# Matmuls on 36, 48 or 64 rows of the array take all 128, over zeros, and a head pair's value products go together

## The chip, the cores and the metric

The kernel runs on one core of a Trainium2 chip. Its time is the device time of one execution in microseconds; the profile is one execution, recorded by the hardware profiler. TensorE (PE) multiplies, with its weight loads shown apart (PEld), VectorE (DVE), ScalarE (ACT) and GpSimd (POOL) do the rest, and SyncE (SP) issues the transfers. Each takes its own instructions in order.

## What is computed

A stack of three layers for 512 tokens of 1024 features in float32: two layers with dilated attention (8 heads of 64) beside an mLSTM (4 heads of 128), then one with a state-space scan (SSD, 16 heads of 64), an attention to the best 128 keys that an indexer (4 heads of 64) picks, and a pooling branch. All have a feed-forward part. Cut to what the change touches:

```
# first block, per head and pattern of dilation
s = einsum('bnqhd,bnkhd->bnhqk', qb, kb) * (Dh ** -0.5)       # scores, Dh = 64
p = exp(s - max(s)); l = sum(p)
o = einsum('bnhqk,bnkhd->bnqhd', p, vb) / l                   # value products
# mLSTM: gate pre-activations mi, mf (4 columns each) of z = h @ w_in + b_in, running maximum m_t
p = exp(dmat - m_t[..., None]) * einsum('bhcld,bhcsd->bhcls', q, k)
# second block
lmat = exp(where(causal, a_cs[l] - a_cs[s], -inf))            # SSD, per head
score = einsum('bqhs,bqh->bqs', relu(einsum('bqhd,bsd->bqhs', qi, ki)), wi * idx_scale)
logits = einsum('bqhgd,bqkhd->bqhgk', qb, ksel) * att_scale   # ksel: keys of the top 128 scores
```

## The kernel before

All products run on TensorE in the float32r format, with each operand split into a first part `h` and a rest `l`; a weight product is three matmuls (`wh` by `h`, `wh` by `l`, `wl` by `h`: lines 280 to 282, or 319 to 321 where the weights move). The backbone is a stream of weight chunks of 128x1024: a transfer (SP queue) into `wr`, the first part on ScalarE (line 250), the rest on VectorE (line 256) or for some on GpSimd (line 254), then 24 matmuls of 512 columns, then an evacuation of the PSUM tile `pb`.

Everything else runs beside that stream as generators: after each K tile of the stream `tick()` lets every generator go on by a fraction of a step (RATE, 0.437 steps a tick for the first attentions, 0.704 for the last), up to its next `yield`. This sets the order in which the program is traced; the tile layer's scheduler then sets the order on each engine. Nothing is reordered at run time.

The pieces that the change touches:

- *Scores.* A head has 64 dimensions. `stack_q` makes a tile A with the head's first part in 64 rows and its rest in the other 64; `stack_k` makes B with the keys' first part in both halves (ScalarE writes one half, line 426, GpSimd copies it to the other, line 427) and writes the keys' rest into the head's own 64 rows of C (line 428). Both heads of a pair share one C. `dots` (lines 434 and 435) is then A by B over 128 rows plus A by C over the head's 64 rows, into one PSUM tile S of n = 128, 256, 384 or 512 columns. Four pairs of heads, two heads each and four query blocks give 32 score pairs in each of the three attentions. The indexer calls `dots` for four heads and the query blocks 1 to 3.
- *After the scores.* VectorE reduces S (line 450), ScalarE takes exp (451), VectorE scales (452, 453), TensorE transposes (462, one 128x128 piece per key block) into PSUM, and VectorE or ScalarE copies to `pt` (470, 468). S, PT, and the other side tiles share two PSUM buffers.
- *Values.* Line 479, for each of four key blocks and both heads: 128 rows, 64 of the output's partitions per head, 512, 384, 256 or 128 columns, with a `yield` after each key block and one split at the end.
- *Broadcasts.* A row held in two float32r parts is spread over 128 partitions by a product with a selecting column (`selr`): `nM` and `fr` of the mLSTM on 36 rows (lines 949 and 1030, per head), `bs` of the SSD on 48 rows (line 1467 per head, 1479 per pair of heads).
- *Gates.* The chunk of the few gate columns carries both parts of the weights side by side; per K tile there is one product on all 128 outputs (line 720) and one on 64 of them (719, 722).

Of the kernel before, what the change touches and what calls it, by code (L numbers as in the profile page):

```python
# [10 lines left out]
F32 = mybir.dt.float32  # L11
F32R = mybir.dt.float32r
# [8 lines left out]
NB = 4  # L21
# [6 lines left out]
# columns between the key blocks of a head's transposed weights  # L28
PTS = 384

# columns of w_in, first block
AQ, AK, AV, MQ, MK, MV, MO, MI, MF, GA, GB = 0, 512, 1024, 1536, 2048, 2560, 3072, 3584, 3588, 3592, 4616
# columns of w_in, second block
# [12 lines left out]
# ---------------------------------------------------------------- constants that depend on shapes alone  # L46
# [31 lines left out]
# ---------------------------------------------------------------- parameters laid out by partition  # L78
# [51 lines left out]
# steps of the work beside the weights per step of the weight stream  # L130
RATE = {"att1": 0.437, "rec": 0.556, "ssd": 0.5, "idx": 0.45, "att2": 0.704, "pool": 0.219}
# gates of the attention's branch that go before its projection
AHEAD = 2
# steps between what one engine prepares and what another one does with it
PAUSE = {"cs": 2, "lf": 5, "cols": 2, "fr": 10, "sum": 1}
# tiles of features that go side by side at the start of a product
LEAD = {"conv": 0, "mo": 0, "ga": 0, "gb": 2, "pa": 2, "pb": 0, "z": 0, "qi": 2, "kv": 2, "q": 2, "br": 2, "up": 2, "u": 2}
# part of the weight chunks whose second part GpSimd works out
SHARE = {"none": 0, "qk": 0.0, "conv": 0.3, "gates": 0.1, "conv2": 0.4, "z": 0.0, "br": 0.2}
# parts in which the first chunks come, and the products before them  # L140
FIRST = [(0, 256), (256, 1024)]
WARM = 36
# the residual's tile before whose preparation the angles of the rotary embedding come
ROPE = 5
# the last product's tiles of features that go over all tokens at once
TAIL = 4
# how far the norms' chains go before what was traced ahead of them
# [3 lines left out]
class Build:  # L151
# [16 lines left out]
    # ---- tiles  # L168
# [26 lines left out]
    # ---- work beside the weight stream: generators that go on a little at each step of it  # L195
# [22 lines left out]
    # ---- a stream of weight chunks, in the order of their use, each split into two float32r parts  # L218
    def chunk(self, key, l, rows, cs, keep=False):
        """one chunk's parts by K tile; with keep, in tiles that last."""  # L220
# [39 lines left out]
    def split(self, src, w=None, n=T):  # L260
        """float32r parts of src (times a per-partition w)."""
        nc = self.nc
        h, lo = self.t("h", F32R), self.t("l", F32R)
        if w is None:
            nc.scalar.activation(h[:, :n], src, AF.Copy)  # L265
            nc.vector.tensor_tensor(lo[:, :n], src, h[:, :n].bitcast(F32), ALU.subtract)  # L266
        else:
            a = nc.scalar.activation(h[:, :n], src, AF.Copy, scale=w)
            b = nc.vector.scalar_tensor_tensor(lo[:, :n], src, w, h[:, :n].bitcast(F32), ALU.mult, ALU.subtract)
            self.last_split = (a, b)  # L270
        return h, lo

    # ---- out[features, tokens]: tiles = [(psum, (wh, wl), first column, columns)], over the K tiles of xs
# [12 lines left out]
    def lin_cols(self, key, l, tiles, xs, evac, lead=0, K0=0):  # L286
        """tiles: lists of up to 128 columns of the weight; evac(j, psum) takes each out. The first
        `lead` tiles go side by side over K, where the last of xs come late."""
# [19 lines left out]
    def lin_tok(self, key, l, cs, xs, evac):  # L308
        """out[tokens, 512 features] by token block."""
# [17 lines left out]
    # ---- a per-token column [128, NB] as rows over all partitions, in PSUM  # L327
# [14 lines left out]
    def colsum(self, tiles):  # L342
        """sums over the partitions (and tiles) by token, as a column [128, NB]."""
# [13 lines left out]
    def rsqrt(self, src, n, scale, tag):  # L357
        """1 / sqrt(src * scale + EPS), or 1 / sqrt(src), by Newton's iteration"""
# [30 lines left out]
    def log1pexp(self, src, dst, rows, n, tag):  # L389
        """dst = max(src, 0) + log1p(exp(-|src|))"""  # L390
# [21 lines left out]
    # ---- heads of 64: [h; l] of one operand against [h; h] of the other over 128 rows, and h against l  # L412
    def stack_q(self, a, x):
        """head x of a pair's tile: its float32r part in its own rows, the rest in the other half."""
# [7 lines left out]
    def stack_k(self, a, x, C):  # L422
        nc = self.nc
        r, o = slice(64 * x, 64 * x + 64), slice(64 - 64 * x, 128 - 64 * x)
        B = self.t("B", F32R)
        nc.scalar.activation(B[r], a[r], AF.Copy)
        nc.gpsimd.tensor_copy(B[o], B[r].bitcast(F32))
        nc.vector.tensor_tensor(C[r], a[r], B[r].bitcast(F32), ALU.subtract)
        return B

    def dots(self, ps, A, B, C, x, c0, n):
        """ps[128, n] = products of the head's columns c0 .. c0 + 128 of A with the first n of B"""
        r = slice(64 * x, 64 * x + 64)
        self.nc.tensor.matmul(ps[:, :n], A[:, c0 : c0 + P], B[:, :n], start=True, stop=False)  # L434
        self.nc.tensor.matmul(ps[:, :n], A[r, c0 : c0 + P], C[r, :n], start=False, stop=True)  # L435

    # ---- softmax attention over key blocks 0..I; heads in pairs that share an output tile
    def attention(self, pairs, prep, V, bias, out):
# [4 lines left out]
        def score(it, x):  # L443
# [3 lines left out]
            self.dots(sp, *qk[pair, x], x, I * P, n)  # L447
# [24 lines left out]
        def value(it):  # L472
            """both heads' products with the values, by key block for all the queries from it on"""
            pair = it[0]
            yp = self.pw.tile([P, T], F32, name=self.name("yp"), tag="yp", bufs=1)
            for J in range(NB):
# [3 lines left out]
                yield  # L480
            out.append(self.split(yp))

# [26 lines left out]
    def conv_silu(self, ps, rbc, nb, w, cb):  # L509
        """silu(causal conv over 4 tokens of ps * rbc, after tokens of the value nb; w [128, 4]).  # L510
        A bias b of the tokens comes as nb = -b, with b times the sum of w in cb."""
# [17 lines left out]
    def setup(self):  # L529
# [6 lines left out]
        # column 127 of ones: its slices are one-hot rows for sums over the partitions  # L536
# [3 lines left out]
        # the tensor engine's clock rises with use: products of zeros until the first operands are there  # L540
# [3 lines left out]
        # the first chunks come by parts: K tiles 0 and 1, then the rest  # L544
# [56 lines left out]
    def norm_in(self, w):  # L601
        """the residual's tiles times w, split, and the sums of their squares."""
# [12 lines left out]
    # ---------------------------------------------------------------- a layer of the first block  # L615
    def hybrid(self, l, xs, acc):
# [11 lines left out]
        # attention: queries and keys with rotary embedding, values by token  # L628
# [44 lines left out]
        C = [None] * 4  # L673

        def prep(i, x):
            if x == 0:
                C[i] = self.t("C", F32R)
            return self.stack_q(qk[i], x), self.stack_k(qk[4 + i], x, C[i]), C[i]
# [16 lines left out]
        # mLSTM: queries, keys, values, gates  # L695
# [13 lines left out]
        # input and forget gates: few columns, so both parts of the weights go as one stationary  # L709
# [7 lines left out]
        for k, (xh, xl) in enumerate(xs):  # L717
            if k > 0:
                nc.tensor.matmul(ps[0:64, :], wh[:, k, 0:64], xl, start=False, stop=False)
            nc.tensor.matmul(ps, wh[:, k, :], xh, start=k == 0, stop=k == 7)  # L720
            if k == 0:
                nc.tensor.matmul(ps[0:64, :], wh[:, k, 0:64], xl, start=False, stop=False)
# [24 lines left out]
        # gated projections of both branches  # L747
# [26 lines left out]
        # the mLSTM's heads, normalised and gated  # L774
# [27 lines left out]
        # feed-forward: relu(y R)^2 = R^2 relu(y)^2, and R^2 goes by token, so it comes in after the second product  # L802
# [33 lines left out]
    def residual(self, w, scale=None):  # L836
        """adds to the residual (times the row of a scale), and prepares its tiles for the next norm by w"""
# [24 lines left out]
    def mlstm(self, it, lf, mqk, mv, res):  # L862
# [3 lines left out]
        # log_sigmoid(f) = -softplus(-f), in columns by token  # L866
# [14 lines left out]
        # within blocks of 128 tokens: b = cumsum(lf); u = i - b; M = running max of u with the carry  # L881
# [15 lines left out]
        # rows of -M, split, for broadcasts  # L897
        yield
        nM = self.t("nM", F32R)[:36]
# [6 lines left out]
        # columns: m = b + M by token, and u with the block decays before query block I  # L906
# [34 lines left out]
        def rowsum(c, src, first, last):  # L941
            """adds the column sums of src to row c of dn"""
# [4 lines left out]
        for h in range(4):  # L947
            bc = self.ps("mbc")
            nc.tensor.matmul(bc, self.sel[0:36, h : h + 1].to_broadcast([36, P]), nM, start=True, stop=True)
# [45 lines left out]
        # rows of den and of num^2 as columns by token  # L995
# [11 lines left out]
        # r = 1 / max(|den|, exp(-m)); the head's norm: r / sqrt(r^2 mean(num^2) + eps)  # L1007
# [14 lines left out]
        fr = self.t("fr", F32R)[:36]  # L1022
# [5 lines left out]
        def out(h):  # L1028
            ps = self.ps("fb")
            nc.tensor.matmul(ps, self.sel[0:36, h : h + 1].to_broadcast([36, P]), fr, start=True, stop=True)  # L1030
# [4 lines left out]
    # ---------------------------------------------------------------- the second block  # L1035
    def second(self, xs, st):
# [4 lines left out]
        # norm of a norm: x' = x R fin with R = 1 / sqrt(a + eps), a the mean of x^2, and x' R' with  # L1041
        # R' = 1 / sqrt(R^2 b + eps), b the mean of (x fin)^2: R R' = 1 / sqrt(b + eps (a + eps))
# [40 lines left out]
        # SSD inputs  # L1083
# [10 lines left out]
        # the SSD branch beside its gate z and the projections of the attention  # L1094
# [39 lines left out]
        # merge of the gated branches  # L1134
# [36 lines left out]
        def pooled(j):  # L1171
            if j == 4:
# [9 lines left out]
        kC = self.t("C", F32R)  # L1182
        kB = [self.stack_k(kv[0], x, kC) for x in range(2)]
# [3 lines left out]
                lambda i, x: (self.stack_q(q[i], x), kB[x], kC),  # L1187
# [19 lines left out]
        # feed-forward, silu(a) * b  # L1207
# [23 lines left out]
        # the last tiles of the last part and the final norm go by halves of the tokens: the first half's norm  # L1231
        # beside the second's products
# [57 lines left out]
    # means over the last 2, 4, 8, 16 tokens, less the token itself, mixed by group  # L1290
    def pool(self, u, yp):
# [5 lines left out]
        # room in the tiles that the attention's transposed weights take later  # L1297
# [302 lines left out]
```

## Time and profile before

| | before |
|---|---|
| median of 3 runs | 2516.99 us (2515.29 to 2517.63) |
| span of the profiled execution | 2514.6 us |
| TensorE busy, share | 2487.1 us, 99% |
| weight loads busy, share | 1944.9 us, 77% |
| VectorE | 1458.1 us, 58% |
| ScalarE | 1006.3 us, 40% |
| GpSimd | 426.5 us, 17% |

The span runs from the first to the last instruction of the profiled execution; the timed runs hold a little more than it. Matmuls are pipelined: one starts before the one ahead of it has ended, so the sum of their durations is larger than the busy time, and what one costs is the step from its start to the next start. A weight load may start while the matmul ahead of it still runs.

### The profile page before, as it was taken

The page shows a single profiled execution, that of the slowest core. Times are in us where ns is not written, and L with a number is a line of the kernel's source. Part 1 is how long each engine was busy: PE and PEld are TensorE (multiplying, and loading weights), DVE is VectorE, ACT ScalarE, POOL GpSimd, SP SyncE. Part 2 cuts the span into 40 slices and gives each one's busy share as a digit, 9 for nine tenths or more (in the row PEclk, how much of TensorE's full clock was granted, in tenths as well). Part 3 has the DMA queues.
Part 4 walks back from the last instruction along what each step waited for, and adds up shares of the span by engine and source line. Part 5 has one row for each costly group of instructions (what it writes and reads, how often), then busy time and mean ns, then how long its engine had stood idle before and what let it go on. Part 6 is the DMA issues. An engine that isn't in the chain of part 4 may idle for free.

```text
span 2514.6 us, 28151 instructions
## 1 busy us (share of the span) xinstructions
PE 2487.1 (99%) x10892; PEld 1944.9 (77%) x10892; DVE 1458.1 (58%) x2428; ACT 1006.3 (40%) x1483; POOL 426.5 (17%) x330
## 2 busy tenths in 40 slices
PE   9999999999999999999999999999999999999998
PEld 8776778888888777778888887767777778888887
DVE  7786655433446577655433447966887655434344
ACT  4566534332233467533332324444324533322222
POOL 4520010000312520011000120343222200101010
PEclk9999999999999999999999999999999999999999
DMA  4221223333223321123233222221221222232222
GB/s 159 86 80 51 68 84 94 101 94 99 93 84 101 93 84 59 52 83 101 84 103 99 93 92 84 84 84 43 84 87 60 68 82 94 93 94 96 96 89 71
DMA packets 63044, 216.45 MB, mean 86 GB/s; under 512 B 7232, under 2 KB 10304, under 8 KB 62912
## 3 DMA queue, kind: packets, MB, share of 16 engines
q1 hardware_dynamic: 60480, 212.14, 26.4%
q8 instruction: 85, 1.39, 0.2%
q10 hardware_dynamic: 2112, 1.48, 0.2%
q0 software_dynamic: 320, 1.05, 0.1%
q14 instruction: 47, 0.39, 0.0%
HBM read 212.55 MB, written 2.10 MB: 85 GB/s over the span
## 4 chain that ended last, share of the span: by engine, by line
PE 90%; DVE 7%; issue 1%; ACT 1%; POOL 0%; POOLq 0%; DVEq 0%; ACTq 0%
PE pb L280 26%; PE pb L282 25%; PE pb L281 25%; DVE wl L256 1%; PE yp L479 1%; DVE cv L522 1%; PE S L435 1%; PE pb L319 1%; PE PT L462 1%; PE pb L320 1%; PE pb L321 1%; PE S L967 1%; PE S L434 1%; PE num L974 1%; DVE sc L1354 1%
## 5 line engine op out<-in xcount | busy, mean ns | idle before, releaser
L280 PE MATMUL pb<-h,wh 128*128 128x512 f32 x2976 | 1206.7, 406 | 1.0 <-DVE tok L668 1.0
L282 PE MATMUL pb<-h,wl 128*128 128x512 f32 x2976 | 1181.3, 397 | 4.8 <-DVE wl L256 4.2
L281 PE MATMUL pb<-l,wh 128*128 128x512 f32 x2976 | 1180.6, 397 | 0.0
L250 ACT ACTIVATE wh<-wr 128x1024 fp32r<-128x1024 f32 (+1 forms) x393 | 410.7, 1054 | 973.9 <-PE pb L281 694.6
L280 PEld LDWEIGHTS pb<-h,wh 128*128 128x128 f32 x2976 | 561.9, 189 | 150.3 <-issue 24.5
L282 PEld LDWEIGHTS pb<-h,wl 128*128 128x128 f32 x2976 | 561.8, 189 | 140.0 <-DVE wl L256 5.5
L281 PEld LDWEIGHTS pb<-l,wh 128*128 128x128 f32 x2976 | 562.3, 189 | 131.0 <-issue 7.7
L256 DVE TENSOR_TENSOR wl<-wr,wh 128x1024 fp32r<-128x1024 f32 (+1 forms) x366 | 480.9, 1318 | 274.5 <-ACT wh L250 271.9
L254 POOL TENSOR_TENSOR wl<-wr,wh 128x1024 fp32r<-128x1024 f32 x27 | 67.3, 2492 | 402.2 <-ACT wh L250 321.4
L826 POOL TENSOR_TENSOR y<-y,rbc 128x512 f32<-128x512 f32 x16 | 24.7, 1541 | 561.2 <-DVE y L824 561.2
L1216 DVE TENSOR_TENSOR f<-pb,rbc 128x512 f32<-128x512 f32 x44 | 30.4, 691 | 123.9 <-PE pb L282 123.9
L265 ACT ACTIVATE h<-f 128x512 fp32r<-128x512 f32 x86 | 54.4, 632 | 109.3 <-DVE f L812 88.2
L1220 POOL TENSOR_TENSOR f<-f,fs 128x512 f32<-128x512 f32 x22 | 38.4, 1744 | 347.6 <-ACT fs L1219 347.6
L266 DVE TENSOR_TENSOR l<-f,h 128x512 fp32r<-128x512 f32 x86 | 59.4, 691 | 44.5 <-ACT h L265 44.5
L834 DVE TENSOR_TENSOR x<-x,pb 128x512 f32<-128x512 f32 x40 | 27.5, 688 | 99.2 <-PE pb L282 99.2
L522 DVE SCALAR_TENSOR_TENSOR cv<-cz,par,cv 128x512 f32<-128x512 f32 x84 | 75.1, 894 | 13.3 <-ACT cv L520 12.1
L451 ACT ACTIVATE s<-s,ng 128x128 f32<-128x128 f32 (+3 forms) x96 | 53.7, 559 | 56.9 <-DVE ng L450 56.4
L824 DVE TENSOR_TENSOR y<-y,pb 128x512 f32<-128x512 f32 x32 | 22.0, 688 | 92.1 <-PE pb L282 92.1
L319 PE MATMUL pb<-wh,h 128*128 128x512 f32 x128 | 51.3, 401 | 0.0
L320 PE MATMUL pb<-wh,l 128*128 128x512 f32 x128 | 50.6, 396 | 0.0
L321 PE MATMUL pb<-wl,h 128*128 128x512 f32 x128 | 50.2, 395 | 0.0
L739 DVE TENSOR_TENSOR gate<-pb,rbc 128x512 f32<-128x512 f32 x40 | 27.3, 687 | 38.7 <-PE pb L282 38.7
(396 smaller groups left out, 2360.9 us busy)
## 6 DMA issues: line engine op xcount, KB each, us to landing
wr<-in_w_dram SPq DMA_DIRECT2D x381, 512.0 KB, 3.5
wr<-in_w_dram SPq DMA_DIRECT2D x16, 448.0 KB, 3.3
x<-in_x_dram SPq DMA_DIRECT2D x8, 256.0 KB, 5.8
out_dram<-o SPq DMA_DIRECT2D x8, 128.0 KB, 2.4
out_dram<-o ACTq DMA_DIRECT2D x8, 128.0 KB, 2.5
wr<-in_w_dram SPq DMA_DIRECT2D x2, 384.0 KB, 5.1
bb<-in_bav_dram POOLq DMA_DIRECT2D x2, 256.0 KB, 3.8
bb<-in_bmv_dram POOLq DMA_DIRECT2D x2, 256.0 KB, 3.6
```

What stands on the lines that cost most here:

```text
L250: nc.scalar.activation(h[:, :n], src, AF.Copy)
L254: nc.gpsimd.tensor_tensor(lo[:, :n], src, h[:, :n].bitcast(F32), ALU.subtract)
L256: nc.vector.tensor_tensor(lo[:, :n], src, h[:, :n].bitcast(F32), ALU.subtract)
L265: nc.scalar.activation(h[:, :n], src, AF.Copy)
L266: nc.vector.tensor_tensor(lo[:, :n], src, h[:, :n].bitcast(F32), ALU.subtract)
L280: mm(ps[:m, :], a, xh, start=k == 0, stop=False)
L281: mm(ps[:m, :], a, xl, start=False, stop=False)
L282: mm(ps[:m, :], b, xh, start=False, stop=k == n - 1)
L319: mm(ps[b], ah, wh[:, kk, :], start=k == 0, stop=False)
L320: mm(ps[b], al, wh[:, kk, :], start=False, stop=False)
L321: mm(ps[b], ah, wl[:, kk, :], start=False, stop=k == 7)
L522: nc.vector.scalar_tensor_tensor(a, z[:, 1 + j : 1 + j + T], w[:, j : j + 1], a, ALU.mult, ALU.add)
```

## The change

Five things change. `stack_k` makes a C of its own for every head, whose other half GpSimd fills with zeros, and `dots` multiplies A by C over all 128 rows. The tiles of the broadcasts are cleared and used on 128 rows in place of 36 or 48; so is `selp`, which ScalarE copies. The gate products of line 719 and 722 take all 128 outputs. In `value`, all eight products of a head pair stand ahead of the first `yield`, and one `yield` follows the split. The comments are gone, so lines move by up to five. The number of matmuls stays.

```
-    def stack_k(self, a, x, C):
+    def stack_k(self, a, x):
...
-        B = self.t("B", F32R)
+        B, C = self.t("B", F32R), self.t("C", F32R)
         nc.scalar.activation(B[r], a[r], AF.Copy)
+        nc.gpsimd.memset(C[o].bitcast(F32), 0.0)
         nc.gpsimd.tensor_copy(B[o], B[r].bitcast(F32))
         nc.vector.tensor_tensor(C[r], a[r], B[r].bitcast(F32), ALU.subtract)
-        return B
-
-    def dots(self, ps, A, B, C, x, c0, n):
-        r = slice(64 * x, 64 * x + 64)
+        return B, C
+
+    def dots(self, ps, A, B, C, c0, n):
         self.nc.tensor.matmul(ps[:, :n], A[:, c0 : c0 + P], B[:, :n], start=True, stop=False)
-        self.nc.tensor.matmul(ps[:, :n], A[r, c0 : c0 + P], C[r, :n], start=False, stop=True)
+        self.nc.tensor.matmul(ps[:, :n], A[:, c0 : c0 + P], C[:, :n], start=False, stop=True)
...
                     nc.tensor.matmul(yp[64 * x : 64 * x + 64, J * P : T], V(h, J), pt, start=J == 0, stop=J == NB - 1)
-                yield
+            yield
             out.append(self.split(yp))
+            yield
...
         for k, (xh, xl) in enumerate(xs):
-            if k > 0:
-                nc.tensor.matmul(ps[0:64, :], wh[:, k, 0:64], xl, start=False, stop=False)
-            nc.tensor.matmul(ps, wh[:, k, :], xh, start=k == 0, stop=k == 7)
-            if k == 0:
-                nc.tensor.matmul(ps[0:64, :], wh[:, k, 0:64], xl, start=False, stop=False)
+            nc.tensor.matmul(ps, wh[:, k, :], xh, start=k == 0, stop=False)
+            nc.tensor.matmul(ps, wh[:, k, :], xl, start=False, stop=k == 7)
...
-        nM = self.t("nM", F32R)[:36]
+        nM = self.t("nM", F32R)
...
-            nc.tensor.matmul(bc, self.sel[0:36, h : h + 1].to_broadcast([36, P]), nM, start=True, stop=True)
+            nc.tensor.matmul(bc, self.sel[:, h : h + 1].to_broadcast([P, P]), nM, start=True, stop=True)
...
-                nc.tensor.matmul(bb, self.sel[0:48, h : h + 1].to_broadcast([48, P]), bs, start=True, stop=True)
+                nc.tensor.matmul(bb, self.sel[:, h : h + 1].to_broadcast([P, P]), bs, start=True, stop=True)
...
-                nc.tensor.matmul(bp, sel[0:48, hp * P : hp * P + P], bs, start=True, stop=True)
+                nc.tensor.matmul(bp, sel[:, hp * P : hp * P + P], bs, start=True, stop=True)
```

`fr` and line 1030 change as `nM` and line 949 do.

The order moves too, in the attentions only. On TensorE at the first pair of the first attention, before (PT are a head's transposes, three key blocks each, pb is the stream):

```order
L282 MATMUL pb_1063<-h_205,wl_1060 128x512
L462 MATMUL PT_1037<-first,s_885 128x128 x3
L280 MATMUL pb_1131<-h_149,wh_1127 128x512
L281 MATMUL pb_1131<-l_150,wh_1127 128x512
L282 MATMUL pb_1131<-h_149,wl_1128 128x512
L280 MATMUL pb_1131<-h_155,wh_1127 128x512
L281 MATMUL pb_1131<-l_156,wh_1127 128x512
L282 MATMUL pb_1131<-h_155,wl_1128 128x512
L462 MATMUL PT_1070<-first,s_901 128x128 x3
```

and now:

```order
L281 MATMUL pb_1069<-l_199,wh_1065 128x512
L464 MATMUL PT_1043<-first,s_888 128x128 x3
L282 MATMUL pb_1069<-h_198,wl_1066 128x512
L464 MATMUL PT_1076<-first,s_904 128x128 x3
L280 MATMUL pb_1069<-h_205,wh_1065 128x512
L436 MATMUL S_1087<-B_962,A_959 128x128
L437 MATMUL S_1087<-C_963,A_959 128x128
```

The second head's transposes stood six stream products behind the first head's and now stand one behind; the first head's come four products earlier. On TensorE at the first value products (yp) of the second block's attention, before:

```order
L435 MATMUL S_14726<-C_14401,A_14583 128x256
L479 MATMUL yp_14736<-pt_2961_14502,vtok_13066 64x512
L479 MATMUL yp_14736<-pt_2963_14512,vtok_13066 64x512
L280 MATMUL pb_14630<-h_11600,wh_14626 128x512
L281 MATMUL pb_14630<-l_11601,wh_14626 128x512
L282 MATMUL pb_14630<-h_11600,wl_14627 128x512
L280 MATMUL pb_14637<-h_11600,wh_14633 128x512
L281 MATMUL pb_14637<-l_11601,wh_14633 128x512
L282 MATMUL pb_14637<-h_11600,wl_14634 128x512
L479 MATMUL yp_14736<-pt_2961_14502,vtok_13066 64x384
L479 MATMUL yp_14736<-pt_2963_14512,vtok_13066 64x384
```

and now:

```order
L437 MATMUL S_14753<-C_14432,A_14610 128x256
L481 MATMUL yp_14763<-pt_2970_14529,vtok_13090 64x512
L481 MATMUL yp_14763<-pt_2972_14539,vtok_13090 64x512
L481 MATMUL yp_14763<-pt_2970_14529,vtok_13090 64x384
L481 MATMUL yp_14763<-pt_2972_14539,vtok_13090 64x384
L481 MATMUL yp_14763<-pt_2970_14529,vtok_13090 64x256
L481 MATMUL yp_14763<-pt_2972_14539,vtok_13090 64x256
L481 MATMUL yp_14763<-pt_2970_14529,vtok_13090 64x128
L481 MATMUL yp_14763<-pt_2972_14539,vtok_13090 64x128
```

The stream products between the key blocks are gone from there; over the whole program the value products stand in 24 pieces before and in 15 now.

## Rows read from the trace of the kernel before

**Rows 1.** The page's first part: busy us, share of the span, instructions.

```profile
PE 2487.1 (99%) x10892; PEld 1944.9 (77%) x10892; DVE 1458.1 (58%) x2428; ACT 1006.3 (40%) x1483; POOL 426.5 (17%) x330
```

**Rows 2.** Waits of the matmul queue: total us, times, longest us.

```profile
PE pb L282 <- DVE wl L256: 4.2, 2, 2.7
...
PE PT L462 <- DVE ng L450: 0.7, 1, 0.7
```

**Rows 3.** Windows, stretch, length, busy us of PE, PEld, DVE, ACT, POOL, clock, DMA.

```profile
83.00:135.00 52.00, 51.31 (x222) 38.67 (x222) 44.17 (x80) 37.05 (x58) 15.89 (x16) 1.00 0.24 82
...
1790.00:1885.00 95.00, 90.47 (x369) 68.34 (x368) 85.45 (x175) 25.01 (x34) 26.55 (x21) 0.99 0.27 86
```

**Rows 4.** Timeline of matmuls (start us, duration us), a score pair of 512 columns.

```profile
109.70 0.40 PE L434 MATMUL S<-B,A 128*128 128x512 f32 x1
110.03 0.50 PE L435 MATMUL S<-C,A 64*128 64x512 f32 x1
110.46 0.50 PE L280 MATMUL pb<-h,wh 128*128 128x512 f32 x1
110.79 0.39 PE L281 MATMUL pb<-l,wh 128*128 128x512 f32 x1
```

**Rows 5.** Timeline of weight loads at the same place.

```profile
109.47 0.19 PEld L434 LDWEIGHTS S<-B,A 128*128 128x128 f32 x1
110.02 0.18 PEld L435 LDWEIGHTS S<-C,A 64*128 64x128 f32 x1 [0.37 <-issue]
```

**Rows 6.** Timeline of matmuls, two side products on full rows.

```profile
300.37 0.39 PE L943 MATMUL dn<-h,hot 128*128 128x512 f32 x1
300.60 0.39 PE L943 MATMUL dn<-l,hot 128*128 128x512 f32 x1
300.83 0.40 PE L280 MATMUL pb<-h,wh 128*128 128x512 f32 x1
```

**Rows 7.** Timeline of matmuls, a score pair of 128 columns.

```profile
85.63 0.22 PE L434 MATMUL S<-B,A 128*128 128x128 f32 x1
85.78 0.32 PE L435 MATMUL S<-C,A 64*128 64x128 f32 x1
86.03 0.50 PE L280 MATMUL pb<-h,wh 128*128 128x512 f32 x1
86.37 0.39 PE L281 MATMUL pb<-l,wh 128*128 128x512 f32 x1
```

**Rows 8.** Timeline of matmuls near the end, full rows, 256 columns.

```profile
2479.77 0.28 PE L1246 MATMUL pb<-h,h 128*128 128x256 f32 x1
2479.88 0.27 PE L1247 MATMUL pb<-l,h 128*128 128x256 f32 x1
```

**Rows 9.** Timeline of matmuls, a broadcast on 48 rows.

```profile
1676.14 0.40 PE L282 MATMUL pb<-h,wl 128*128 128x512 f32 x1
1676.47 0.50 PE L1467 MATMUL bb<-bs,selr 48*128 48x512 f32 x1
1676.90 0.50 PE L280 MATMUL pb<-h,wh 128*128 128x512 f32 x1
1677.24 0.39 PE L281 MATMUL pb<-l,wh 128*128 128x512 f32 x1
```

**Rows 10.** Groups by line and shape: count, busy us, mean ns, idle before.

```profile
L435 PE MATMUL S<-C,A 64*128 64x512 f32 x24 | 11.9, 495 | 0.0
```

**Rows 11.** Timeline of matmuls, gate products in a row.

```profile
140.81 0.39 PE L720 MATMUL pb<-h,wh 128*128 128x512 f32 x1
141.03 0.40 PE L719 MATMUL pb<-l,wh 128*64 128x512 f32 x1
141.27 0.39 PE L720 MATMUL pb<-h,wh 128*128 128x512 f32 x1
```

**Rows 12.** GpSimd: the memset of nM (ns), and its timeline at the first pair.

```profile
L900 POOL MEMSET nM<- x2: 523/523/523, 169.0 to 940.8; 36x512 f32 x2
...
82.94 0.61 POOL L427 CAST B<-B 64x512 fp32r<-64x512 f32 x1 [2.71 <-ACT B L426]
```

More of the change, by code (lines that the diff above doesn't have):

```diff
@@ L446, in score @@
             sp = self.ps("S")
-            self.dots(sp, *qk[pair, x], x, I * P, n)
+            self.dots(sp, *qk[pair, x], I * P, n)
             s = self.t("s")
@@ L671, in tok @@
             self.lin_tok("w_in", l, cols(col, T), xs, ev)
-        C = [None] * 4
         def prep(i, x):
-            if x == 0:
-                C[i] = self.t("C", F32R)
-            return self.stack_q(qk[i], x), self.stack_k(qk[4 + i], x, C[i]), C[i]
+            return self.stack_q(qk[i], x), *self.stack_k(qk[4 + i], x)
         av = []
@@ L1021, in mlstm @@
             nc.tensor.transpose(tp[0:4, B * P : B * P + P], f[:, 4 * B : 4 * B + 4], idn)
-        fr = self.t("fr", F32R)[:36]
+        fr = self.t("fr", F32R)
         nc.gpsimd.memset(fr.bitcast(F32), 0.0)
@@ L1029, in out @@
             ps = self.ps("fb")
-            nc.tensor.matmul(ps, self.sel[0:36, h : h + 1].to_broadcast([36, P]), fr, start=True, stop=True)
+            nc.tensor.matmul(ps, self.sel[:, h : h + 1].to_broadcast([P, P]), fr, start=True, stop=True)
             return nums[h], ps
@@ L1181, in second @@
         ya = []
-        kC = self.t("C", F32R)
-        kB = [self.stack_k(kv[0], x, kC) for x in range(2)]
+        kk = [self.stack_k(kv[0], x) for x in range(2)]
         att = self.start(
@@ L1186, in second @@
                 [(i, 4 + i) for i in range(4)],
-                lambda i, x: (self.stack_q(q[i], x), kB[x], kC),
+                lambda i, x: (self.stack_q(q[i], x), *kk[x]),
                 lambda h, J: vtok[:, J * P + 64 * (h // 4) : J * P + 64 * (h // 4) + 64],
@@ L1340, in indexer @@
                 sp = self.ps("is")
-                self.dots(sp, qA[h], B, C, h % 2, I * P, n)
+                self.dots(sp, qA[h], B, C, I * P, n)
                 wcol = wi[:, 4 * I + h : 4 * I + h + 1]
@@ L1390, in ssd @@
             nc.tensor.matmul(br[0:16, c * P : c * P + P], a[:, c * 16 : c * 16 + 16], tri, start=True, stop=True)
-        bs = self.t("bs", F32R)[:48]
+        bs = self.t("bs", F32R)
         nc.gpsimd.memset(bs.bitcast(F32), 0.0)
@@ L1399, in ssd @@
             sel = self.t("selp", F32R)
-            src = self.c("sel")[0:48, 8 * gi : 8 * gi + 8].unsqueeze(2).to_broadcast([48, 8, 64])
-            nc.scalar.activation(sel[0:48, :].rearrange("p (h d) -> p h d", d=64), src, AF.Copy)
+            src = self.c("sel")[:, 8 * gi : 8 * gi + 8].unsqueeze(2).to_broadcast([P, 8, 64])
+            nc.scalar.activation(sel.rearrange("p (h d) -> p h d", d=64), src, AF.Copy)
             tp = self.ps("tp")
```

## Prediction

> **What bounds the kernel now.** I read the page first. TensorE is busy 99% of the span [rows 1], and the waits of the matmul queue are few: the largest named one is 4.2 us, the one inside the attention 0.7 us [rows 2]. So the time is the sum of the steps from one matmul's start to the next, almost everywhere. The two stretches to distrust are those in which VectorE is nearly as busy: 44.17 of 52 us at the head of the first attention, 85.45 of 95 us beside the indexer [rows 3]. There a faster TensorE may meet work that is not ready.
>
> Then I read TensorE's order of time at the places that the change touches. Look at the distance between starts, not at the durations: neighbouring matmuls overlap. A full-row product of 512 columns takes a step of 0.23 us, also where two side products stand in a row [rows 6]. A score pair of 512 columns (line 434 on 128 rows, line 435 on 64) takes 0.33, then 0.43, and the stream product behind it 0.33 more: 1.09 us from 109.70 to 110.79 [rows 4], where three steps of 0.23 would be 0.69. The weight loads show why [rows 5]: the load for line 434 starts at 109.47, a whole product ahead of its matmul, whereas the load for line 435 starts at 110.02, with its matmul, after the engine sat idle for 0.37 us. A load for fewer rows does not run ahead of the product before it, nor does the full-row load behind it run ahead of the small one.
>
> **The change part by part.** The forecast is a sum of removed steps, each priced by such a place.
>
> *Price of one product on few rows.* At 512 columns: 1.09 - 0.69 = 0.40 us [rows 4, 6]. At 128 columns the same three starts are 85.63 to 86.37, 0.74 us [rows 7]. A full-row product of 128 columns in this form has no row; its nearest is one of 256 columns with a step of about 0.12 us [rows 8] (the loads, 0.19 us each in rows 5, overlap one another there). So 0.74 - 0.12 - 0.12 - 0.23 = 0.27 us; the bounds are 0.40, if 128 columns cost half of that, and 0.1, if these products had to go one load at a time (0.74 - 0.19 - 0.19 - 0.23). Sizes 256 and 384 lie between 0.27 and 0.40; I take 0.335. A broadcast on 48 rows, 1676.14 to 1677.24, takes 1.10 us for three steps [rows 9]: 0.40 again.
>
> *Score pairs.* There are 24 of each of four sizes (four pairs of heads, two heads, three attentions); x24 at 512 columns in [rows 10]. 24 x (0.40 + 0.335 + 0.335 + 0.27) = 24 x 1.34 = 32.2 us. About nine of them stand directly beside value products in the new order, which stay on 64 of the array's columns and keep a change of their own; 0.1 us each comes off (the first of the three excesses, 0.33 - 0.23 [rows 4, 6]). Left: 31 us.
>
> *Indexer.* Four heads by three key blocks: 4 x (0.40 + 0.335 + 0.335) = 4.3 us of TensorE. But VectorE has only 9.5 of 95 us idle there [rows 3], and it makes both the choice of the keys and the second parts of the weights, for which the product of line 282 waits 4.2 us [rows 2]. Bounds 0 and 4.3; I take 2.
>
> *Broadcasts.* 16 of line 1467 (one per head), and 8 each of lines 949, 1030 and 1479 (four heads in two layers, twice; eight head pairs): 40 x 0.40 = 16 us. Two pairs of line 1030 stand side by side and share a change; I take 15.
>
> *Gate products.* Here 64 of the outputs are used, not 64 of the rows. The steps into such a product and out of it are 0.22 and 0.24 us [rows 11], those of the stream. So widening the 16 of them (eight K tiles, two layers) to 128 outputs gives 0 us. The Trainium skill, "TensorEngine Tiling (Array Packing)", Tiling Modes and Key Properties, counts 128 rows by 64 columns as a tiling of its own and says that a change of mode drains the engine; by it these 16 products would be worth some 16 x 0.40 = 6 us more and the time would be 2466. The rows say no, and the sum goes by them.
>
> *Value products.* A pair's eight products (four key blocks, two heads) stand in 24 pieces in 12 runs of the old order and in 15 pieces of the new one: nine fewer breaks. A break costs between 0 and the 0.40 of a whole change there and back [rows 4, 6]; at 0.25, nearer to the upper end since the products still use another shape than the stream, it is 2 us.
>
> *What is added.* 18 memsets of 64x512 on GpSimd, nearest row 0.523 us for 36x512 [rows 12]: 9 us in all. GpSimd's queue holds the memset ahead of the copy that fills B; but that copy waits for ScalarE's part of B (2.71 us at the first pair [rows 12]), and the memset does not, so it goes in that wait: 0 us, at most 0.5 us at the head of each of the three attentions if the tile for C comes free late. The wider memsets of nM, fr and bs clear more rows at once, the same 512 elements per row: 0.
>
> *Where a gain is given back.* TensorE comes to each transposed weight, score tile or weight part earlier than before, and VectorE does the same work as before. At the first pair the second head's transposes already waited 0.7 us [rows 2] and the new order puts them one stream product behind the first head's, where six stood. All three attentions begin like this. I take off 5 us for new waits (bounds 0 and 16, the latter half of the scores' 31).
>
> Sum: 31 + 2 + 15 + 0 + 2 - 5 = 45 us. The profiled span is 2514.6 us, the median 2516.99; the 2.4 us between them are not touched. 2514.6 - 45 + 2.4 = 2472 us.
>
> **The rivals.**
>
> *VectorE sets the pace.* The score chain (reduce, exponential, scale, copy) runs on VectorE beside the convolution, and at the head of the attention VectorE is 85% busy [rows 3]. If half of the scores' gain and all of the indexer's turns into waits, the gain is 15.5 + 15 + 2 = 32.5: 2484 us. Against it: TensorE was busy 51.31 of the same 52 us [rows 3], so it waited under 1 us.
>
> *All of it arrives.* No new waits, the indexer's 4.3 in full and 0.40 at every score size: 24 x 1.60 + 4 x 1.2 + 15 + 2 = 60, less 1 for neighbours: 2458 us.
>
> *The change does not do what it says.* The late load could come with something that stays: the accumulation into the same bank, or the broadcast operand. Then only the 2 us of the value products are left: 2515 us. Against it: the two products of line 943 also follow each other into one bank, at 0.23 [rows 6], and 48-row broadcasts and 64-row scores show the same three excesses [rows 4, 9].
>
> *A load of full rows is the one that waits.* If a load could run beside a matmul only on other rows, every one of the 148 widened products would expose its load of 0.19 us [rows 5] instead: 148 x 0.19 = 28 us slower, 2545. Against it: the load at 109.47 runs beside a product on the same rows [rows 5]. The Trainium skill, "TensorE: Matmul & The Clock Gate", Part 3 (The mechanism), says that loads overlap with matmuls in flight only when the row group differs; this trace disagrees.
>
> *Slower: the transposes wait.* TensorE takes its work in order. If each of the 96 groups of transposes came to its operand or its PSUM tile 0.69 us too early, as the one in rows 2 did, 96 x 0.69 = 66 us would be lost in place of 5: 2472 + 61 = 2533 us. It decides from (45 + 5) / 96 = 0.52 us on average. For it: the pairs of transposes stand closer now. Against it: one wait in 96 before.
>
> **How the numbers follow.** Forecast 0.66; VectorE's pace 0.19; all of it 0.09; no effect 0.03; full-row loads 0.01; transposes 0.02. The range takes in the first three cases with their unknown prices: 2457 to 2486; what is left out is the last three and the edges. A difference under 0.2% (5 us) cannot be told from no change here: faster 0.94, same 0.03, slower 0.03.
>
> **What would show it.** In the profile after: the second score product's load starting with the product before it, and steps of 0.23, 0.23, 0.23 at 512 columns and 0.12 or less at 128; a lone broadcast within 0.69 us for three steps; the gate products unchanged at 0.23; value products in one run with an excess at each end only. Wrong prices show as other steps there; wrong cover as idle time of TensorE released by VectorE in the two stretches of rows 3, above all at transposes and at line 282's products.

## The result and the profile after

The changed kernel took 2478.62 us (2476.51 to 2479.92) beside 2517.14 us for the kernel before on the same chip: a ratio of 0.9849 [0.9835, 0.9863], or 38.5 us less. Forecast were 2472 us, 45 us less, with 2457 to 2486 as the range. The direction, the mechanism and the range held; the forecast was 6.6 us too low. The profiled execution has a span of 2478.1 us.

The page's line of busy times, after (beside rows 1):

```profile
PE 2442.3 (99%) x10892; PEld 1950.7 (79%) x10892; DVE 1457.4 (59%) x2428; ACT 1005.0 (41%) x1483; POOL 438.7 (18%) x348
```

With the same 10892 matmuls TensorE is busy 44.8 us less, and the span is 36.5 us shorter. The difference is idle time: 2514.6 - 2487.1 = 27.5 us before, 2478.1 - 2442.3 = 35.8 us now. So some 8 us of what the products gave came back as waits. Slower steps took a further part: the mean granted clock of TensorE is 0.994 in this execution and 0.996 in the one before, by estimate 2478 x 0.006 - 2515 x 0.004 = 5 us (the changed kernel's other three executions of that comparison show 0.995 and 0.996).

TensorE in order of time, after, at a score pair of 512 columns (start, duration, engine, line, operands; compare rows 4):

```profile
108.05 0.39 PE L436 MATMUL S<-B,A 128*128 128x512 f32 x1
108.28 0.40 PE L437 MATMUL S<-C,A 128*128 128x512 f32 x1
108.52 0.40 PE L280 MATMUL pb<-h,wh 128*128 128x512 f32 x1
108.76 0.40 PE L281 MATMUL pb<-l,wh 128*128 128x512 f32 x1
```

Read the starts: 0.23, 0.24, 0.24 from line 436 to line 281, where 0.33, 0.43, 0.33 stood. The weight load of line 437 there (compare rows 5):

```profile
108.05 0.19 PEld L437 LDWEIGHTS S<-C,A 128*128 128x128 f32 x1
```

It starts at 108.05, with the product before its own, a whole product ahead. That is the sign that the prediction named.

A pair of 128 columns, after (compare rows 7), and then a broadcast (compare rows 9):

```profile
85.95 0.22 PE L436 MATMUL S<-B,A 128*128 128x128 f32 x1
86.01 0.27 PE L437 MATMUL S<-C,A 128*128 128x128 f32 x1
86.12 0.45 PE L280 MATMUL pb<-h,wh 128*128 128x512 f32 x1
86.41 0.39 PE L281 MATMUL pb<-l,wh 128*128 128x512 f32 x1
...
1660.69 0.40 PE L282 MATMUL pb<-h,wl 128*128 128x512 f32 x1
1660.92 0.40 PE L1462 MATMUL bb<-bs,selr 128*128 128x512 f32 x1
1661.16 0.40 PE L280 MATMUL pb<-h,wh 128*128 128x512 f32 x1
1661.40 0.39 PE L281 MATMUL pb<-l,wh 128*128 128x512 f32 x1
```

The short pair takes 86.41 - 85.95 = 0.46 us for three steps in place of 0.74, the broadcast 0.71 in place of 1.10.

What came back: TensorE's named waits, after (engine, tile and line that waited, what released it: us in all, times, longest):

```profile
PE PT L464 <- DVE ng L452: 6.0, 3, 3.6
PE pb L282 <- DVE wl L256: 5.2, 4, 2.7
```

In rows 2 the transposes waited once, for 0.7 us. They wait for line 452's reduction of the score tile on VectorE, now for 6.0 us, and 3.6 of that stand at one place, the first pair of the first attention. VectorE and then TensorE there:

```profile
117.33 1.64 DVE L419 TENSOR_TENSOR A<-qk,A 64x512 fp32r<-64x512 f32 x1
118.98 1.12 DVE L430 TENSOR_TENSOR C<-qk,B 64x512 fp32r<-64x512 f32 x1
120.11 0.69 DVE L452 CUSTOM_DVE_ANT_0 s<-S,const 128x512 f32<-128x512 f32 x1
```

```profile
120.87 0.90 PE L464 MATMUL PT<-first,s 128*128 128x128 f32 x3 [3.58 <-DVE ng L452]
...
123.91 0.63 PE L282 MATMUL pb<-h,wl 128*128 128x512 f32 x1
124.34 0.63 PE L280 MATMUL pb<-h,wh 128*128 128x512 f32 x1
```

VectorE splits the next pair's queries and keys (lines 419 and 430, 2.76 us) ahead of the reduction on which the transposes rest. And once TensorE goes on, a step takes 0.43 in place of 0.23. The stretches of that place, first of the changed kernel, then of the kernel before (stretch, length, busy time and count of PE, PEld, DVE, ACT and POOL, granted clock, DMA share, GB/s):

```profile
121.00:124.50 3.50, 3.50 (x13) 3.03 (x14) 2.39 (x5) 2.15 (x6) 0.00 (x0) 0.50 0.00 0
124.50:128.00 3.50, 3.50 (x14) 2.80 (x13) 3.39 (x7) 2.67 (x3) 1.00 (x2) 0.69 0.00 0
```

```profile
123.00:126.50 3.50, 3.44 (x16) 2.73 (x17) 3.43 (x9) 2.85 (x5) 0.00 (x0) 1.00 0.00 0
```

A granted clock of 0.50 is the lower of the two levels, 1.2 GHz. Counted from the rows, 3.5 x (1 - 0.50) + 3.5 x (1 - 0.69) = 2.8 us go there besides the 3.6 us of the wait.

### The profile page after: what moved, and what is told of

Read it like the earlier page. It is cut to its first block, busy times and chain, and to the rows that moved or that the text cites. A ratio compares the mean times of both kernels' runs of the same rounds, so it can differ in the third digit from the quotient of the medians.

```text
span 2478.1 us, 28176 instructions
## 1 busy us (share of the span) xinstructions
PE 2442.3 (99%) x10892; PEld 1950.7 (79%) x10892; DVE 1457.4 (59%) x2428; ACT 1005.0 (41%) x1483; POOL 438.7 (18%) x348
## 5 line engine op out<-in xcount | busy, mean ns | idle before, releaser
L830 DVE TENSOR_TENSOR x<-x,pb 128x512 f32<-128x512 f32 x40 | 27.5, 688 | 99.3 <-PE pb L282 99.2
L266 DVE TENSOR_TENSOR l<-f,h 128x512 fp32r<-128x512 f32 x86 | 59.4, 690 | 44.8 <-ACT h L265 44.8
```

## The experiments

Theory: a product on 36, 48 or 64 rows lengthens the three steps around it, by about 0.4 us together, and full rows take that away; a part comes back where VectorE is late. Rival: the new order, not the rows, makes the gain; or one of the five edits makes it alone.

**1. The score products alone, and the same order without the rows.** `e1_scores` is the edit of `stack_k` and `dots` alone. `e9_order_only` is the same kernel, memsets and own C included, with the second product back on 64 rows; TensorE, VectorE, ScalarE and GpSimd have the same order in both.

```
# e9_order_only against e1_scores
+        r = slice(64 * x, 64 * x + 64)
-        self.nc.tensor.matmul(ps[:, :n], A[:, c0 : c0 + P], C[:, :n], start=False, stop=True)
+        self.nc.tensor.matmul(ps[:, :n], A[r, c0 : c0 + P], C[r, :n], start=False, stop=True)
```

> Scores and indexer alone take 128 rows (a C of its own per head, its other half cleared); broadcasts, gates and value products as before. By the sum of steps, 35 us less before anything is given back (31 and 4.3). Theory A, the give-back comes with the new order of VectorE and TensorE: 2517 - 35 + 8 = 2490 us, and the 3.6 us wait of the transposes at the first pair is there. Theory B, the give-back comes because TensorE arrives earlier: also about 2490, but then the same edit without the wider product (the next kernel) costs nothing.

> As the kernel of the scores alone, with the same order on every engine, but the second score product stays on 64 rows; so it has the new order, the memsets and the extra tiles and none of the gain. Theory A (order): slower than before by the waits, 3 to 8 us, 2520 to 2525, with a wait of a few us of the transposes at the first pair. Theory B (pace): the same as before within 1 us, and the difference to the kernel of the scores is only about 27 us in place of 35.

Measured, beside 2518.63 us of the kernel before: `e1_scores` 2495.35, 0.9904 [0.9887, 0.9921]; `e9_order_only` 2524.78, 1.0024 [1.0012, 1.0036]. The rows alone, in one order, are worth 29.4 us (the slowest run of `e1_scores` took 2496.9 us, the fastest of `e9_order_only` 2520.99); what the edit brings besides them costs 6.2 us (3.0 to 9.1 by the interval). The rival falls: the order makes nothing, it costs. `e1_scores` is 5 us slower than both theories expected. The pages of e9 and then e1:

```profile
PE 2493.2 (99%) x10892; PEld 1945.9 (77%) x10892; DVE 1456.6 (58%) x2428; ACT 1006.6 (40%) x1483; POOL 437.0 (17%) x348
```

```profile
PE 2459.6 (99%) x10892; PEld 1945.0 (78%) x10892; DVE 1456.0 (58%) x2428; ACT 1003.9 (40%) x1483; POOL 437.0 (18%) x348
```

From e9 to e1 TensorE is busy 33.6 us less, while its idle time rises from 2522.6 - 2493.2 = 29.4 to 2495.1 - 2459.6 = 35.5 us. So 6.1 us came back because TensorE arrives earlier, beside what the order costs. As the order is the same, the steps of the two traces can be compared matmul by matmul: the steps at the 108 widened products and next to them are 35.7 us shorter in e1, all others together 8.2 us longer, the 6.1 us of idle time among them. Part of what the order costs has a place. TensorE of e9 at the first pair, then the stretch behind it:

```profile
122.62 0.67 PE L463 MATMUL PT<-first,s 128*128 128x128 f32 x3 [2.81 <-DVE ng L451]
```

```profile
122.62:125.60 2.98, 2.98 (x11) 2.40 (x12) 2.52 (x5) 1.98 (x5) 0.00 (x0) 0.55 0.00 0
```

The wait is there without any row widened: 2.8 us, 2.1 more than the 0.7 of rows 2, and 2.98 x 0.45 = 1.3 us go by the clock behind it. That is 3.4 of the 6.2; the rest has no place yet. In e1 the same wait is 3.60 us. Over the whole profile e9 idles only 29.4 - 27.5 = 1.9 us more than the kernel before, and is busy 2493.2 - 2487.1 = 6.1 us more: most of the difference stands as longer steps, not as waits.

**2. The broadcasts alone.** The diff for `bs`; `nM`, `fr` and `selp` go the same way. The order stays as before.

```
-        bs = self.t("bs", F32R)[:48]
+        bs = self.t("bs", F32R)[:128]
-                nc.tensor.matmul(bb, self.sel[0:48, h : h + 1].to_broadcast([48, P]), bs, start=True, stop=True)
+                nc.tensor.matmul(bb, self.sel[0:128, h : h + 1].to_broadcast([128, P]), bs, start=True, stop=True)
```

> The broadcasts alone take 128 rows; the order of the instructions is that of before. 40 products at 0.40 us less what neighbours share: 15 us, 2502, if nothing is given back. If a faster TensorE alone brings new waits (theory B), 5 to 8 us of it come back beside the state-space scan: 2507 to 2510.

Measured: 2506.83, 0.9954 [0.9939, 0.9969], 11.8 us less. The number is close to theory B's, but waits of 5 us are not there: TensorE idles 2504.1 - 2475.6 = 28.5 us, 1 us more than before. The order is that of before, so the steps can be compared again: those at the 40 broadcasts and next to them are 13.2 us shorter. Most lone broadcasts give the 0.4 that was forecast (0.37 to 0.40); two that stand behind value products give 0.2 each, and two that stand together give less than two lone ones. TensorE at such a pair, before, then in `e2_broadcasts`:

```profile
315.76 0.40 PE L281 MATMUL pb<-l,wh 128*128 128x512 f32 x1
316.09 0.73 PE L1030 MATMUL fb<-fr,selr 36*128 36x512 f32 x2
...
317.09 0.39 PE L280 MATMUL pb<-h,wh 128*128 128x512 f32 x1
```

```profile
314.62 0.40 PE L281 MATMUL pb<-l,wh 128*128 128x512 f32 x1
314.91 0.72 PE L1030 MATMUL fb<-fr,selr 128*128 128x512 f32 x2
...
315.70 0.39 PE L280 MATMUL pb<-h,wh 128*128 128x512 f32 x1
```

From line 281 to line 280 it was 1.33 us and is 1.08: 0.25 us for two, where two lone ones would give 0.80.

**3. The value products alone, and the gate products alone.**

```
# e3_values
-                yield
+            yield
             out.append(self.split(yp))
+            yield
# e4_gates
-            if k > 0:
-                nc.tensor.matmul(ps[0:64, :], wh[:, k, 0:64], xl, start=False, stop=False)
-            nc.tensor.matmul(ps, wh[:, k, :], xh, start=k == 0, stop=k == 7)
-            if k == 0:
-                nc.tensor.matmul(ps[0:64, :], wh[:, k, 0:64], xl, start=False, stop=False)
+            nc.tensor.matmul(ps, wh[:, k, :], xh, start=k == 0, stop=False)
+            nc.tensor.matmul(ps, wh[:, k, :], xl, start=False, stop=k == 7)
```

> The value products of a head pair go together, two steps of the generator fewer per pair; all else as before. Fewer breaks: 2 us less, 2515. Rival: the denser pace of the attention brings waits that are larger than this, 2518 to 2522.

> The gate products alone take all 128 outputs; the order is that of before. By the steps of the trace they cost the same: within 1 us of the kernel before. If 128 rows by 64 outputs were a shape that costs a change, 16 x 0.40 = 6 us less, 2511.

Measured: values 2516.17 beside 2518.63, 0.9990 [0.9981, 0.9999], about 2.5 us less; gates 2517.17 beside 2518.99, 0.9997 [0.9987, 1.0006], no change that can be told. The three edits that count sum to 23.3 + 11.8 + 2.5 = 37.6 us, the whole change gave 38.5: no effect of one on another shows, though the intervals leave room for a few us. Nor does one edit alone make the gain. A run of value products in the changed kernel, with the stream around it:

```profile
185.91 0.40 PE L282 MATMUL pb<-h,wl 128*128 128x512 f32 x1
186.24 2.37 PE L481 MATMUL yp<-pt,tok 128*64 128x512 f32 x16
188.54 0.50 PE L280 MATMUL pb<-h,wh 128*128 128x512 f32 x1
188.88 0.39 PE L281 MATMUL pb<-l,wh 128*128 128x512 f32 x1
```

Sixteen stand in a row here. The step into them is 0.33 and the first step behind them 0.34, against 0.23: an excess of about 0.1 at each end. The row shows the sixteen as one and hides two more. By their own starts in the trace, the first two of 512 columns take 0.48 us together and the next two 0.43; the last two of 128 columns take 0.21 and the two ahead of them 0.11. So a break costs about 0.35 us here.

**4. How few rows are few?** The full change with 96 rows in place of 128 for the broadcasts.

```
-        bs = self.t("bs", F32R)
+        bs = self.t("bs", F32R)[:96]
...
-                nc.tensor.matmul(bb, self.sel[:, h : h + 1].to_broadcast([P, P]), bs, start=True, stop=True)
+                nc.tensor.matmul(bb, self.sel[0:96, h : h + 1].to_broadcast([96, P]), bs, start=True, stop=True)
```

`nM`, `fr` and `selp` go the same way.

> The changed kernel with the broadcasts on 96 rows in place of 128 (the order is the same). If any load on fewer than all rows stays behind the product ahead of it, the steps around a broadcast are 0.33, 0.43, 0.34 again and the time is about 12 us over the changed kernel, 2490. If only 64 rows and fewer do, the steps are 0.23 and the time is 2478.

Measured in one execution: 2478.38 us. TensorE at a broadcast of it, then the broadcast's weight load:

```profile
1659.32 0.40 PE L282 MATMUL pb<-h,wl 128*128 128x512 f32 x1
1659.56 0.41 PE L1460 MATMUL bb<-bs,selr 96*128 96x512 f32 x1
1659.80 0.39 PE L280 MATMUL pb<-h,wh 128*128 128x512 f32 x1
```

```profile
1659.33 0.19 PEld L1460 LDWEIGHTS bb<-bs,selr 96*128 96x128 f32 x1
```

Steps of 0.24 on both sides, and the load starts with the product before its own: 96 rows behave as 128 do. So the array need not be filled; 36, 48 and 64 rows cost (the pair above, rows 9, rows 4), 96 do not, and what lies between 64 and 96 was not tried.

**5. Taking the wait at the first pair away.** Two ways on the full change: fewer steps of the attention per K tile (`e7_rate`), and the reduction moved up in the scheduler's order (`v3_prio`).

```
# e7_rate
-RATE = {"att1": 0.437, ..., "att2": 0.704, ...}
+RATE = {"att1": 0.397, ..., "att2": 0.64, ...}
# v3_prio
+PRIO = 60
-            nc.vector.tensor_tensor_reduce(s[:, :n], sp[:, :n], bias(I), -1.0, 3e38, ALU.add, ALU.min, ng)
+            with self.tc.high_priority(offset=PRIO):
+                nc.vector.tensor_tensor_reduce(s[:, :n], sp[:, :n], bias(I), -1.0, 3e38, ALU.add, ALU.min, ng)
```

> The changed kernel, with the attentions' generators slower by the share of steps that the value products gave up (0.397 for 0.437, 0.64 for 0.704), so that they end where they ended before. If the denser pace of the attention makes the waits, they fall and the time is 3 to 6 us under the changed kernel, 2473 to 2476. If the waits hang on single places of the order, the time is within 3 us of 2478.6 either way.

> The changed kernel, with VectorE's reduction of each score tile raised in the scheduler's priority by 60, so that at the first pair it stands before the next pair's A and C in VectorE's order, where the changed kernel has it behind them. If the give-back of the order comes from that place, the 3.6 and 1.7 us waits of the transposes shrink to under 1 us, the clock does not fall there, and the time is 4 to 8 us under the changed kernel: 2471 to 2475. If VectorE simply has no room, the wait moves to another instruction and the time stays within 2 us of 2478.6.

Measured beside 2518.99 us: `e7_rate` 2477.47, 0.9834 [0.9820, 0.9849]; `v3_prio` 2473.32, 0.9819 [0.9803, 0.9836]. VectorE in `v3_prio` at the first pair, and TensorE:

```profile
116.62 0.68 DVE L452 CUSTOM_DVE_ANT_0 s<-S,const 128x512 f32<-128x512 f32 x1
...
117.23 0.69 DVE L452 CUSTOM_DVE_ANT_0 s<-S,const 128x512 f32<-128x512 f32 x1
...
117.95 0.69 DVE L420 TENSOR_TENSOR A<-qk,A 64x512 fp32r<-64x512 f32 x1
```

```profile
117.36 0.55 PE L464 MATMUL PT<-first,s 128*128 128x128 f32 x3 [1.84 <-DVE ng L452]
```

Both reductions stand ahead of the split of A now, and the wait is 1.84 us in place of 3.58, not under 1 us as expected. The wait of 1.65 us in the second layer is gone, but one at the second block's attention grew from 0.75 to 1.71 us; in all the transposes wait 3.6 us over two, where it was 6.0 over three. The time came out as expected. With the slower rate the waits of the transposes fall too, to 3.2 us over four, yet its time is that of the change within the intervals: TensorE idles 2478.0 - 2441.9 = 36.1 us in it, beside 35.8 in the change, so the waits moved. Where to was not followed.

**6. Again, with more rounds and with the edits together.** The change and `v3_prio`'s kernel once more on one chip; `v5_prio_rate` adds `e7_rate`'s numbers to the raised priority, `v6_prio_pace` the old number of steps in `value` (four `yield`s ahead of the split, none behind).

> The changed kernel as it is, beside the next ones on one chip: 2478 to 2479 us, as before.

> The changed kernel with VectorE's reductions of the scores raised by 60: 2473 us again, 5 us under the changed kernel in the same runs, if the gain of the first run was real.

> The raised reductions and the slower pace (0.397 and 0.64) together. If both take away different waits, 2470 to 2472; if they take away the same ones, 2473.

> The raised reductions, with the value products together but the old number of generator steps per head pair (four before the split). If the shorter attention costs nothing any more, 2473 as without it; if the old pace is the better cover, 2470 to 2472.

Measured beside 2517.72 us: the change 2478.64, 0.9845 [0.9831, 0.9858]; raised priority 2473.32, 0.9826 [0.9813, 0.9840]; with the rates 2475.84, 0.9832 [0.9819, 0.9846]; with the old steps 2474.92, 0.9825 [0.9811, 0.9839]. The raised priority gave 2473.32 both times, some 5 us under the change. The intervals of the two ratios overlap, but the runs on this chip do not (2472.46 to 2477.38, the change 2478.14 to 2480.56): that it is faster is shown, by how much is less sure. The other two missed what was expected and add nothing that can be told. The raised priority alone is the best of the versions run.

## Why the prediction was right, and by how much not

- *The mechanism* stood: the load, the steps at 512 and 128 columns and at the broadcast came nearly as written (0.71 us for the 0.69 of a broadcast), the load for full rows runs beside a product on the same rows, and 29.4 us follow from the rows alone in one order. That 96 rows do as well was not foreseen; the prediction spoke of fewer rows in general. The rivals that the change does nothing, and that full rows expose their loads, are out.
- *The price by size.* 0.40 at 512 columns was 0.39, 0.27 at 128 was 0.28. The straight line between them was wrong: at 384 columns it is 0.39, not 0.335, and at 256 the median of the 24 pairs is 0.38. The rows at 384, before and then after (from line 434 to 281, 0.97 us; from line 436 to 281, 0.58):

```profile
100.16 0.34 PE L434 MATMUL S<-B,A 128*128 128x384 f32 x1
100.43 0.43 PE L435 MATMUL S<-C,A 64*128 64x384 f32 x1
100.79 0.50 PE L280 MATMUL pb<-h,wh 128*128 128x512 f32 x1
101.13 0.39 PE L281 MATMUL pb<-l,wh 128*128 128x512 f32 x1
```

```profile
98.90 0.33 PE L436 MATMUL S<-B,A 128*128 128x384 f32 x1
99.07 0.34 PE L437 MATMUL S<-C,A 128*128 128x384 f32 x1
99.25 0.39 PE L280 MATMUL pb<-h,wh 128*128 128x512 f32 x1
99.48 0.39 PE L281 MATMUL pb<-l,wh 128*128 128x512 f32 x1
```

- *Score pairs, indexer and new waits*, 31 + 2 - 5 = 28 us, came to 23.3 (20 to 28.5 by the interval of e1). The prices were right in sum: 35.7 us of steps in one order, where the prediction had 31 and 4.3. The step that was mis-sized is "I take off 5 us for new waits" (7.3 with the 2.3 us taken off the indexer): by e9 the order costs 6.2 us even with the old rows, and another 6.1 us of idle time come with TensorE's earlier arrival, some 12 us. The place was named (VectorE, the transposes at the head of the attention). The size was not: the prediction priced the wait by the 0.7 us of rows 2 and looked at TensorE's order alone, not at what VectorE has ahead of the reduction, nor at the clock behind the wait.
- *Broadcasts*: 11.8 us (7.8 to 15.4) for the 15 forecast. The price of a lone one, from rows 9, held, and so did the 1 us taken off for the two pairs, which saved some 0.5 in place of 1.6. Left out were the neighbours that are not the stream (the steps sum to 13.2) and 1 us of new idle time.
- *Value products*: 2 forecast, about 2.5 measured (0.2 to 4.8). That they are so close is partly luck. A break costs about 0.35 and not 0.25, and the count of 24 and 15 pieces leaves out the places where only score products stand between: with them the traces have 28 pieces before and 16 now, twelve breaks fewer in place of nine. That would be 4.2 us, still within the interval.
- *Gates*: 0 forecast, and the interval of e4, 1.5 us slower to 3.3 us faster, leaves out 6 us; the steps of rows 11 said so. The Trainium skill ("TensorEngine Tiling (Array Packing)", Tiling Modes) says that a change of tiling mode drains TensorE; at these products no run shows it.
- *Memsets*: nothing, as forecast, as far as can be told. The changed kernel's row on GpSimd:

```profile
L428 POOL MEMSET C<- 64x512 f32 x18 | 9.5, 527 | 39.7 <-ACT e L961 37.5 <-PE pb L282 0.9 <-PE S L436 0.5
```

  9.5 us of work, where the prediction had 9 from rows 12. No run had the memsets without the order, so that they cost nothing is read from the profile, not tested.
- *The rivals.* "VectorE sets the pace" had the right direction and came nearer: 2478.6 lies between its 2484 and the forecast's 2472, 5.4 us from the one and 6.6 from the other. The named waits of the transposes are for VectorE, as it said. Its premise that half of the scores' gain is lost was too much: 12 us of 35.3 came back, part of it by the order. "All of it arrives", 2458 us, needed no new waits. "The transposes wait" would have meant 66 us of waits at 96 groups; it is 6.0 us at three.

## What to carry to other kernels

A product on 36, 48 or 64 rows alone between full-row ones cost 0.3 to 0.4 us more here than one on 128 rows, although it has less to do; padding it with zeros (here to 96 or 128 rows) takes that away, if another engine has the time to clear the tile. Look for it in the starts of consecutive matmuls and in loads that start with their own product, and price a lone one and a neighbour of its like apart. Before taking off "waits" by feel, read the late engine's queue at the first place where the faster engine arrives, and see what stands ahead of the operand.

## What the runs showed of the hardware beyond that

The granted clock behind a wait differs between executions of one kernel. Two profiles of the kernel with the raised priority, `v3_prio` and then `v3_again`, each over the 3.5 us behind the same wait of 1.84 us:

```profile
117.36:120.86 3.50, 3.50 (x13) 2.87 (x14) 3.37 (x6) 3.45 (x7) 1.69 (x3) 0.60 0.51 150
```

```profile
118.04:121.54 3.50, 3.01 (x16) 2.30 (x17) 3.37 (x6) 3.44 (x7) 1.69 (x3) 1.00 0.50 150
```

The other engines' work is the same, but the first is at a clock of 0.60 and has 13 matmuls in the stretch, the second is at 1.00 and has 16. Behind the wait of 3.58 us the changed kernel's second profile, that of `after_again`, shows 0.50 as the first does. In the second layer of the changed kernel the same transposes wait 1.65 us (the wait, then the stretch behind it), and the clock stays:

```profile
885.13 0.55 PE L464 MATMUL PT<-first,s 128*128 128x128 f32 x3 [1.65 <-DVE ng L452]
```

```profile
885.10:888.50 3.40, 3.37 (x19) 2.93 (x20) 3.33 (x7) 3.39 (x8) 0.00 (x0) 1.00 0.00 0
```

So a wait can cost its own length and most of it again in slow steps behind it: 2.8 us behind the 3.58. What decides whether it does is left open.
